# A decoder layer on one core: gates, broadcasts, branch stores and weight loads on other DMA queues

## The chip, the cores and the metric

The kernel runs on one core of one Trainium2 chip. The metric is the device time of one execution in microseconds; lower is better. The kernel before was timed three times, with a median of 1371.44 us (1367.7 to 1374.45). The profile comes from one further execution of 1372.67 us.

## What is computed

The input x has 2048 rows of 1024 float32 values. One layer is computed:

```
h    = rms_norm(x, norm_g);  proj = h @ w_in            # 1024 -> 3592 columns
fox  : 8 heads of 64, q and k normed per head, causal softmax attention with a bias
       c[t] - c[s], where c is the running sum of log_sigmoid(h @ w_f + b_f)
pool : 4 groups of 64 columns: trailing mean over 2/4/8/16 rows minus the row,
       times w_pool (64 x 64 per group), times pool_scale
sb   : 4 heads of 64, stick-breaking attention: A[t,s] = sigmoid(z_ts) prod_{s<j<t}(1 - sigmoid(z_tj)), s < t
mixed = concat(fox * silu(fg), pool * silu(pg), sb * silu(sg))
out   = x + mixed @ w_out
```

## The kernel before, in words

Rows are cut into 16 tiles of 128. Every large product is made in pairs of float16 numbers (a high and a low part), three matmuls for one. The work goes in five parts that overlap: fox heads 0 to 3 ("a"), fox heads 4 to 7 ("b"), the stick-breaking heads ("s"), the pooled branch ("p", whose tiles are strewn into the projections of s) and the output projection ("o"). Tiles and tensors carry these letters in their names: `tta` belongs to a, `ttb` to b, `tts` to s.

**One tile of attention.** `proj` (L322) makes q, k, v and the gate of a tile. `stacks` puts k and q side by side (`st`), has them transposed by a DMA from SyncE's queue (`qT`, L482) and lets GpSimd place them (L485, L487). `qk` makes scores on TensorE (L420, `sp`). In a and b VectorE adds the running sums `negc` (L754) and ScalarE takes the exponential (L764). In s ScalarE takes the sigmoid (L889), GpSimd masks the diagonal block (`affine_select`, L891, with the memset L892), VectorE multiplies along the row (the scan, L897), and GpSimd keeps the last value (`left`, L901). Then `split_t` makes high and low halves (L446 on ScalarE, L449 on VectorE) in `pp` and has them transposed by a DMA from SyncE's queue into `tt` (L451), and `pv` multiplies with v (L463 to L465). Scores run ahead of `pv` by three heads. There are four `tt` buffers.

**What lies in DRAM between the parts.** Gates go to `gat` (`keep_gate`, L509), right after the ScalarE instruction that scales them (L508). Branch results go to `mix` (`send`, L791 for a and b, L920 for s, L1013 for the pooled branch). The running sums of a tile are stored as rows (`cd`, L581) and read back, broadcast to all 128 partitions, into `negc` (`spread`, L662). The output part reads `mix` and `gat` of a tile (L1034, L1036), multiplies (L1039, L1041), has it transposed (`xTm`, L379), multiplies with w_out and adds x.

**Weights.** The weights of b, s, p and o are read twice by `raw` (L240; for p L960 and L961): once while an earlier part runs, to measure them (`wm`), and once to scale and split them (`wr`). Both go through the three buffers `raw`, which the rows of x share. The weights of p are first folded with w_pool, stored (L956) and read back; `wpT` (L945) feeds that.

**What sets the order.** Each engine has one queue and works it off in order, DMA issues included: a DMA that must wait holds back what stands behind it. The order within a queue is chosen when the program is built, by a planner that simulates the times of all instructions (`schedule_with_timeline_sim=True`); `later` and `tick` delay some steps by a number of projection steps. The constants `QW`, `QGAT`, `QSPR`, `QMIX` and others name the engine whose queue a DMA is put on ('y' SyncE, 's' ScalarE, 'g' GpSimd); `dq` looks them up.

Of the kernel before, what the change touches and what calls it, by code (L numbers as in the profile page):

```python
# [84 lines left out]
XB = 2  # L85
HPX = (0, 0, 0, 0, 0)
QB4 = 'y'
QW = 'y'
QPARK = 's'
QLX = 's'  # L90
QGAT = 'y'
QCD = 'g'
QSPR = 'y'
QMIX = 'y'
QOL = 'y'
QOR = 'y'
QOUT = 'y'
# [29 lines left out]
def hybrid(ctx: ExitStack, tc, xN, w_in, w_pT, w_out, ng, b_f, qg, kg, w_pool, p_scale, bands, out):  # L127
# [22 lines left out]
    def dq(k):  # L150
        return {"y": sy, "s": s, "g": g}[k]
# [3 lines left out]
    def later(k, fn):  # L155

        if k:
            waiting.append([k, fn])
        else:
            fn()  # L160
# [69 lines left out]
    class Weights:  # L230
# [6 lines left out]
        def raw(self, kt, a, what):  # L237
            c = self.c0 + sum(self.widths[:a])
            wr = xp.tile([P, self.widths[a]], F32, name=f"{what}{self.name}_{kt}_{a}", tag="raw", bufs=LX)
            dq(QW).dma_start(wr, self.src[kt * P:(kt + 1) * P, c:c + self.widths[a]])  # L240
            return wr
# [259 lines left out]
    def keep_gate(ph, i, j, src, iw, c):  # L501
# [5 lines left out]
        with first(HGT):  # L507
            s.activation(gt, src, AF.Copy, scale=iw[:, 0:1])  # L508
        later(GTD, lambda: dq(QGAT).dma_start(gat[j][:, c:c + 256], gt))  # L509


    class Fox:
# [143 lines left out]
        def spread(self, j):  # L656
# [4 lines left out]
            def send():  # L661
                dq(QSPR).dma_start(negc[:, :, blk], cd[j][h0:h0 + NH, :].partition_broadcast(P))  # L662
                spread_.add(f"{self.ph}_{NT - 1 - j}")
# [117 lines left out]
        def pv(self, i, h, parts, rl):  # L781
# [4 lines left out]
            if h == NH - 1:  # L786
# [3 lines left out]
                def send():  # L790
                    dq(QMIX).dma_start(mix[j][:, c:c + 256], om)  # L791
                    mixed.add((self.ph, j))
# [8 lines left out]
    class Stick(Fox):  # L801
# [102 lines left out]
        def pv(self, i, h, parts, left):  # L904
# [7 lines left out]
            if h == NH - 1:  # L912
# [6 lines left out]
                def send():  # L919
                    dq(QMIX).dma_start(mix[j][:, c:c + 256], om)  # L920
                    mixed.add((self.ph, j))
# [4 lines left out]
    class Pool:  # L926
# [9 lines left out]
        def fold(self, kt):  # L936

            w = self.w
            if kt == 0:
# [3 lines left out]
                for k in range(2):  # L943
                    self.wts.append(big.tile([P, D], F32, name=f"wpT{k}", tag="KV"[k], bufs=(KB, VB)[k]))
                    dq(QW).dma_start(self.wts[k], w_pT[k])  # L945
                self.folded = []
# [8 lines left out]
            self.folded.append(dr.tile([P, 256], F32, name=f"wf{kt}", tag=f"wf{kt}"))  # L955
            dq(QMIX).dma_start(self.folded[kt], fq)  # L956

            def raw(kt, a, what):
                wr = xp.tile([P, 512], F32, name=f"{what}p_{kt}", tag="raw", bufs=LX)
                dq(QW).dma_start(wr[:, 0:256], self.folded[kt])  # L960
                dq(QW).dma_start(wr[:, 256:512], w.src[kt * P:(kt + 1) * P, w.c0 + 256:w.c0 + 512])  # L961
                return wr
# [33 lines left out]
        def pool(self, i):  # L996
# [15 lines left out]
            def send():  # L1012
                dq(QMIX).dma_start(mix[j][:, 512:768], ym)  # L1013
                mixed.add(("p", j))
# [308 lines left out]
```

## Time and profile before

| | |
|---|---|
| median of 3 runs | 1371.44 us |
| profiled execution | 1372.67 us, its span 1371.0 us |
| mean granted TensorE clock | 0.945 |
| PE / DVE / ACT / POOL busy | 88% / 73% / 57% / 20% of the span |
| DMA queue of SyncE (q1) | 576480 packets, 232.59 MB |
| DMA queue of ScalarE (q10) | 10832 packets, 33.67 MB |
| DMA queue of GpSimd (q0) | 512 packets, 0.07 MB |

Engines: PE is TensorE's matmuls, DVE VectorE, ACT ScalarE, POOL GpSimd, SP SyncE, which only issues DMAs here. SPq, ACTq and POOLq are the issuing sides of these engines. The chain of waits goes back from the last instruction, at each step to what released it. "Issue" in it is time in which an engine waited for nothing that the profile shows. Times of a transfer "to landing" count from its issue.

### The profile page before, as it was taken

The page shows a single profiled execution, that of the slowest core. Times are in us where ns is not written, and L with a number is a line of the kernel's source. Part 1 is how long each engine was busy: PE and PEld are TensorE (multiplying, and loading weights), DVE is VectorE, ACT ScalarE, POOL GpSimd, SP SyncE. Part 2 cuts the span into 40 slices and gives each one's busy share as a digit, 9 for nine tenths or more (in the row PEclk, how much of TensorE's full clock was granted, in tenths as well). Part 3 has the DMA queues.
Part 4 walks back from the last instruction along what each step waited for, and adds up shares of the span by engine and source line. Part 5 has one row for each costly group of instructions (what it writes and reads, how often), then busy time and mean ns, then how long its engine had stood idle before and what let it go on. Part 6 is the DMA issues. An engine that isn't in the chain of part 4 may idle for free.

```text
span 1371.0 us, 27421 instructions
## 1 busy us (share of the span) xinstructions
PE 1202.0 (88%) x10380; PEld 653.9 (48%) x10380; DVE 996.3 (73%) x2069; ACT 776.5 (57%) x1457; POOL 274.0 (20%) x440
## 2 busy tenths in 40 slices
PE   6979987898896698997988879999998899878998
PEld 3445544555454354554544435545454454443443
DVE  4778876878876466878888656768786888956641
ACT  5678866868665366666667645546554556412210
POOL 0212221111011111121111034423331113303300
PEclk9989998999998899999999889999999999999999
DMA  6569998789999999989899998799798789999763
GB/s 221 162 144 209 206 197 174 171 192 196 246 197 201 218 203 192 219 168 182 173 241 187 174 208 172 170 194 182 159 196 176 159 197 259 234 266 293 210 181 93
DMA packets 587956, 268.07 MB, mean 196 GB/s; under 512 B 523440, under 2 KB 561712, under 8 KB 587824
## 3 DMA queue, kind: packets, MB, share of 16 engines
q1 hardware_dynamic: 576480, 232.59, 81.0%
q10 hardware_dynamic: 10832, 33.67, 7.8%
q8 instruction: 81, 1.33, 0.4%
q14 instruction: 51, 0.42, 0.1%
q0 software_dynamic: 512, 0.07, 0.0%
HBM read 102.60 MB, written 34.67 MB: 100 GB/s over the span
## 4 chain that ended last, share of the span: by engine, by line
PE 50%; DMA 20%; issue 10%; DVE 10%; ACT 6%; POOL 2%; SPq 1%; ACTq 0%; POOLq 0%; DVEq 0%
PE pr L322 11%; DMA ttb<-ppb 8%; DMA tta<-ppa 7%; DVE rrs L897 5%; PE pqkb L322 5%; PE pvgb L322 5%; PE pvga L322 4%; PE pqka L322 3%; PE spb L420 3%; PE pqks L322 3%; PE pvgs L322 2%; PE spa L420 2%; PE pp L322 2%; PE sps L420 1%; DMA xTm<-ppm 1%
## 5 line engine op out<-in xcount | busy, mean ns | idle before, releaser
L322 PE MATMUL pr<-wo,xTm 128*128 128x512 f16 x768 | 173.1, 387 | 15.5 <-DMA xTm<-ppm 13.8
L446 ACT CAST pps<-rrs 128x640 f16<-128x640 f32 (+7 forms) x96 | 76.1, 795 | 115.2 <-DVE rrs L897 97.9
L897 DVE TENSOR_TENSOR_SCAN rrs<-rrs 128x640 f32<-128x640 f32 (+7 forms) x64 | 105.3, 1651 | 40.8 <-POOL rrs L891 30.9
L322 PEld LDWEIGHTS <-xTm 128*128 128x128 f16 x768 | 75.4, 99 | 107.7 <-DMA xTm<-ppm 15.3
L322 PEld LDWEIGHTS <-xTs 128*128 128x128 f16 x768 | 76.0, 101 | 98.4 <-issue 22.3
L764 ACT ACTIVATE Lb<-Lb,nmb 128x640 f32<-128x640 f32 (+7 forms) x96 | 85.6, 893 | 59.6 <-DVE nmb L758 59.4
L322 PEld LDWEIGHTS <-xTb 128*128 128x128 f16 x768 | 74.1, 100 | 88.3 <-issue 10.0
L322 PEld LDWEIGHTS <-xTx 128*128 128x128 f16 x720 | 69.3, 100 | 79.0 <-issue 7.8
L322 PE MATMUL pqks<-ws,xTs 128*128 128x512 f16 x384 | 98.8, 403 | 7.1 <-DVE vo L345 5.8
L449 DVE TENSOR_TENSOR pps<-rrs,pps 128x640 f16<-128x640 f32 (+7 forms) x96 | 88.9, 937 | 20.0 <-ACT pps L446 19.5
L764 ACT ACTIVATE La<-La,nma 128x640 f32<-128x640 f32 (+7 forms) x96 | 85.4, 891 | 29.6 <-DVE nma L758 29.2
L463 PE MATMUL ob<-Vb,ttb 128*128 128x64 f16 x544 | 62.7, 199 | 44.5 <-DMA ttb<-ppb 43.7
L449 DVE TENSOR_TENSOR ppb<-Lb,ppb 128x640 f16<-128x640 f32 (+7 forms) x96 | 89.6, 952 | 11.1 <-ACT ppb L446 10.7
L449 DVE TENSOR_TENSOR ppa<-La,ppa 128x640 f16<-128x640 f32 (+7 forms) x96 | 89.2, 947 | 10.6 <-ACT ppa L446 10.2
L322 PE MATMUL pvgs<-ws,xTs 128*128 128x512 f16 x384 | 94.2, 388 | 1.6 <-DVE ym L1010 1.6
L754 DVE CUSTOM_DVE_ANT_0 Lb<-spb,negcb,c 128x640 f32<-128x640 f32 (+7 forms) x64 | 60.2, 945 | 47.7 <-PE spb L420 28.9
L322 PE MATMUL pvgb<-wb,xTb 128*128 128x512 f16 x384 | 93.0, 388 | 1.7 <-ACT gta L508 1.7
L322 PE MATMUL pqkb<-wb,xTb 128*128 128x512 f16 x384 | 92.6, 387 | 0.7 <-DVE wb L281 0.7
L889 ACT ACTIVATE rrs<-sps,nc 128x640 f32<-128x640 f32 (+7 forms) x96 | 80.0, 862 | 23.3 <-PE sps L420 23.1
L322 PE MATMUL pp<-auxp,xTp 128*128 128x512 f16 x384 | 92.2, 387 | 0.7 <-DVE vo L345 0.6
L463 PE MATMUL oa<-Va,tta 128*128 128x64 f16 x544 | 60.2, 199 | 32.7 <-DMA tta<-ppa 32.5
L420 PE MATMUL spa<-Ka,qTa 128*128 128x512 f16 (+3 forms) x320 | 78.0, 358 | 8.6 <-DVE mma L754 6.5
(312 smaller groups left out, 3053.5 us busy)
## 6 DMA issues: line engine op xcount, KB each, us to landing
xn<-in_xN_dram SPq DMA_DIRECT2D x16, 512.0 KB, 5.1
xTd<-xTx ACTq DMA_DIRECT2D x16, 512.0 KB, 4.6
xTb<-xTd ACTq DMA_DIRECT2D x16, 512.0 KB, 5.0
xTs<-xTd ACTq DMA_DIRECT2D x16, 512.0 KB, 4.5
xTp<-xTd ACTq DMA_DIRECT2D x16, 512.0 KB, 5.0
go<-gat SPq DMA_DIRECT2D x16, 512.0 KB, 7.6
mt<-mix SPq DMA_DIRECT2D x16, 512.0 KB, 5.3
xr<-in_xN_dram SPq DMA_DIRECT2D x16, 512.0 KB, 4.0
```

Of the source, the lines that this page charges most:

```text
L322: t.matmul(psum, x[:, xa, kt, :], wt[:, wa, c0:c0 + n], start=(kt == 0 and i == 0), stop=(kt == KT - 1 and i == 2))
L420: t.matmul(sp[:, b - c0 + off:e - c0 + off], qT[:, a * NH + h, :], Kc[b // 512][:, h, b % 512:b % 512 + e - b], start=(a == 0), stop=(a == ...
L446: s.copy(hi, p32)
L449: lo_eng.tensor_tensor(lo, p32, hi, ALU.subtract)
L463: t.matmul(o, tt[:, b, :], vh[:, 0:HD], start=first, stop=False)
L754: v.tensor_tensor_reduce(lt, sp, negc[:, h, c0:c1_], c1[:, 0:1], 4 * NEG if a == 0 else mm[:, a - 1:a], ALU.add, ALU.max, mm[:, a:a + 1])
L764: s.activation(ls[a], ls[a], AF.Exp, bias=nm[:, 0:1], accum_out=la[:, a, h:h + 1])
L889: s.activation(gg, sp, AF.Sigmoid, scale=self.nc2[:, 0:1])
L897: v.tensor_tensor_scan(gg, gg, gg, init, ALU.mult, ALU.bypass)
```

## The change

Four constants change; no other line does. The 64 gate stores leave SyncE's queue for ScalarE's. The 32 broadcasts, the 64 stores of branch results, the 8 stores of the folded pool weights and the 82 loads of weights leave it for GpSimd's, where so far the 16 stores of `cd` were the only DMAs.

```diff
-QW = 'y'
+QW = 'g'
...
-QGAT = 'y'
+QGAT = 's'
 QCD = 'g'
-QSPR = 'y'
-QMIX = 'y'
+QSPR = 'g'
+QMIX = 'g'
```

## Rows read from the trace of the kernel before

**Rows 1.** The page's head and its busy times.
```profile
span 1371.0 us, 27421 instructions
...
PE 1202.0 (88%) x10380; PEld 653.9 (48%) x10380; DVE 996.3 (73%) x2069; ACT 776.5 (57%) x1457; POOL 274.0 (20%) x440
```

**Rows 2.** The chain of waits by line, in 50:442, 442:800 and 800:1180.
```profile
by line: DMA tta<-ppa 24.5%; PE pvga L322 13.7%; PE pqka L322 12.0%; PE spa L420 7.8%; issue 7.0%; PE oa L463 3.1%; ACT La L764 3.1%; PE oa L464 2.4%; PE oa L465 2.4%; PE pvgb L322 2.4%; DVE La L754 2.2%; ACT ppa L446 2.1%; DMA xTd<-xTx 1.3
...
by line: DMA ttb<-ppb 30.1%; PE pqkb L322 16.8%; PE pvgb L322 14.9%; PE spb L420 12.5%; PE pvgs L322 5.2%; PE ob L463 4.2%; PE ob L464 3.4%; PE ob L465 3.4%; PE pqks L322 3.4%; DVE ppb L449 1.1%; PE pq L949 1.0%; issue 1.0%; PE spb L422 0.8
...
by line: issue 26.5%; DVE rrs L897 17.0%; PE pqks L322 7.5%; PE pp L322 7.0%; PE sps L420 4.3%; DMA tts<-pps 4.1%; ACT rrs L889 3.8%; PE pvgs L322 3.7%; POOL rrs L891 2.6%; DVE pps L449 2.4%; ACT pps L446 2.1%; PE pr L322 2.0%; POOL qTs L48
```

**Rows 3.** Waits of PE: us in total, times, longest us.
```profile
PE ob L463 <- DMA ttb<-ppb: 43.7, 21, 8.2
PE oa L463 <- DMA tta<-ppa: 32.5, 20, 4.9
...
PE os L463 <- DMA tts<-pps: 11.1, 5, 5.6
```

**Rows 4.** Waits of SP's queue, in the same columns.
```profile
SPq L451 <- PE sps L420: 54.7, 29, 10.0
SPq L451 <- DVE ppb L449: 44.1, 27, 4.5
...
SPq L662 <- DMA cd<-cr: 29.2, 11, 6.5
...
SPq L1013 <- DVE auxp L345: 25.1, 7, 6.4
SPq L509 <- ACT auxp L508: 15.4, 11, 3.8
...
SPq L240 <- DVE ppx L345: 12.9, 8, 3.2
```

**Rows 5.** Issues by line: duration ns min/median/max, first and last start us.
```profile
L509 SPq DMA_DIRECT2D gat<-gta x16: 320/447/751, 36.5 to 365.0; - x16
...
L791 SPq DMA_DIRECT2D mix<-omb x16: 327/575/1071, 450.2 to 801.7; - x16
...
L1013 SPq DMA_DIRECT2D mix<-ym x16: 319/322/1003, 894.5 to 1182.5; - x16
...
L451 SPq DMA_TRANSPOSE ttb<-ppb x94: 1188/1782/5882, 439.5 to 792.7; - x94
...
L581 POOL DMA_DIRECT2D cd<-cr x16: 518/563/702, 42.5 to 361.7; - x16
...
L401 ACTq DMA_DIRECT2D xTs<-xTd x16: 326/326/340, 673.6 to 1103.8; - x16
```

**Rows 6.** DMA issues: count, KB each, median us to landing.
```profile
gat<-auxp SPq DMA_DIRECT2D x29, 128.0 KB, 2.6
...
cd<-cr POOLq DMA_DIRECT2D x16, 4.0 KB, 3.5
```

**Rows 7.** POOL's instructions from 1032 us: start us, us, [idle before <-releaser].
```profile
1032.13 0.65 POOL L891 TENSOR_SCALAR_AFFINE_SELECT rrs<-rrs 128x128 f32<-128x128 f32 x1 [4.74 <-ACT rrs L889]
...
1036.81 0.69 POOL L901 COPY left<-rrs 128x1 f32<-128x1 f32 x1 [4.00 <-DVE rrs L897]
...
1041.09 0.29 POOL L891 TENSOR_SCALAR_AFFINE_SELECT rrs<-rrs 128x128 f32<-128x128 f32 x1 [3.01 <-ACT rrs L889]
```

**Rows 8.** SP's queue at the start of b, in the same columns.
```profile
450.80 5.60 SPq L662 DMA_DIRECT2D negcb<-cd  x6
456.51 4.99 SPq L451 DMA_TRANSPOSE ttb<-ppb  x2
...
463.56 3.85 SPq L662 DMA_DIRECT2D negcb<-cd  x6
```

**Rows 9.** Stage a: us, PE, PEld, DVE, ACT, POOL busy, clock, DMA share, GB/s.
```profile
50.00:442.00 392.00, 335.10 (x3328) 193.66 (x3327) 307.62 (x881) 275.60 (x582) 64.03 (x88) 0.94 0.92 194
```

**Rows 10.** ACT's instructions around one gate of b.
```profile
510.22 0.47 ACT L508 ACTIVATE gtb<-pvgb,iwb 128x256 f32<-128x256 f32 x1
510.59 0.82 ACT L764 ACTIVATE Lb<-Lb,nmb 128x640 f32<-128x640 f32 x1
```

## The prediction

> **What bounds the kernel now.** I read the page's busy times first, then the chain of waits cut into stages, then who waits for whom on PE and on SP, then the lengths of the issues, and last the order of POOL's and SP's instructions in two short stretches. The span is 1371.0 us and POOL is busy for 274.0 of them [rows 1]; the profiled execution itself took 1372.67 us, 1.67 more than its span and 0.1% over the median of the runs, 1371.44. The sums below are made on 1372.67.
>
> The chain of waits shows three different kernels. In stage a (50 to 442 us) the landing of the transposes tta makes up 24.5% of the chain, in stage b (442 to 800 us) that of ttb 30.1%, and the rest of stage b is almost only matmuls; neither shows POOL in its leading lines. In stage s (800 to 1180 us) tts is down to 4.1%, while 26.5% is "issue", 17.0% the scan L897 on DVE, and POOL's mask rrs L891 2.6% [rows 2]. PE agrees: it idles 43.7 us for ttb and 32.5 for tta, but only 11.1 for tts [rows 3]. So in a and b a transpose that leaves SP earlier is worth something, at most the 76 us that PE idles there. In stage s it is worth next to nothing.
>
> What that "issue" of stage s is, POOL's order tells [rows 7]: mask (L891), then the one-column copy L901 after 4.00 us of waiting for DVE's scan, then the next mask after 3.01 us of waiting for ACT's sigmoid. POOL does its work strictly in order, and the next scan cannot start before the mask. Any instruction put between L901 and L891 that waits or takes time moves the mask, and with it the scan. That is the point on which I decide.
>
> **What leaves SP.** 250 DMAs: 64 gates (to ACT), 64 stores of branches, 8 of the folded pool weights, 32 broadcasts and 82 loads of weights (to POOL). By their start times 64 of them are issued in stage a, 109 in b, 77 in s. An issue on SP takes from 0.322 us (ym) to 0.575 (omb); I take the 0.447 of gta [rows 5], which gives 29, 49 and 35 us. To these come the waits that stand ahead of them on SP, and hold back what is queued behind: 29.2 us of broadcasts for the landing of cd and 12.9 of loads for ppx, both in stage a; 25.1 of ym's stores and 15.4 of gates in stage s [rows 4]. SP gets back 71 us in a, 49 in b, 75 in s.
>
> How much of it reaches the end? If each us delays a transpose, the share of the chain that runs through transposes counts: 71 x 0.245 = 17, 49 x 0.301 = 15, 75 x 0.041 = 3, together 35 us. But SP often has nothing to send: its transposes wait 54.7 us for PE sps (a landing buffer still being read, in stage s) and 44.1 for their own data from ppb [rows 4]. When SP waits for its own data anyway, freed time is empty time. I take a little over half: **-20 us** (bounds -35 and 0). At the start of b the effect is plainest: two runs of six broadcasts hold SP for 5.60 and 3.85 us while ttb transposes wait behind them [rows 8].
>
> **What comes to POOL.** 186 DMAs. The only row of such an issue on POOL is cd's, 0.563 us for 8 rows of 512 bytes; the moved ones have 128 rows, the broadcasts 512 pieces. Bounds: 0.56 us, and the 1.782 us of a ttb transpose on SP [rows 5], which has far more pieces. I take 0.9, nearer to the row of the same queue.
>
> In stage s it is 48 of them (16 oms, 16 ym, 8 wmo, 8 wro): 43 us (27 to 86). The 25.1 us for which SP waited ahead of ym's stores goes along, since POOL's queue is as strictly ordered. Of these 68 us about 30% is on the path (issue 26.5% with the mask's 2.6%, rounded): **+20 us** (bounds 27 x 0.30 = +8, and 86 plus both waits of stage s, 40, x 0.30 = +38). Behind the waiting store stand the mask, the copy of `left` and the placing of K; DVE's scan waits for the first, ACT's and DVE's splitting for the scan, SP's transpose for these.
>
> In a and b 138 come, 124 us, where POOL is busy 64.03 of 392 us in stage a [rows 9] and off the chain. The cover is POOL's idleness; it fails where the waiting broadcasts meet the placing of K (L485, L487), for which PE's scores wait. Twelve broadcasts in a row at 0.56 to 1.78 us are 7 to 21 us in front of one K copy at the start of b. **+4 us** (0 to +15).
>
> At this price the Trainium skill speaks against the change a second time: "SBUF — State Buffer", section "SBUF: two separate sides", says that DMAs from GpSimd's queue have their descriptors written by that engine, which VectorE can lock out during certain operations, so that they start late. Stage a does not bear it out: cd's sixteen issues stay between 518 and 702 ns [rows 5] while DVE is busy 307.62 of 392 us [rows 9]. In stage s a one-column copy on POOL takes 0.69 us [rows 7], so something like it may hold there; another 0.5 us on each of the 48 issues would make it 48 x 0.5 x 0.30 = 7 us more, 1391.
>
> **What comes to ACT.** A gate's store must wait until its own ACTIVATE of 0.47 us has ended, where the next one now starts 0.37 after it [rows 10]; then the issue takes the 0.326 us of an xTs load [rows 5]. That is 0.43 us lost for each gate, 28 us for 64. ACT's leading lines hold 5.2% of the chain in a, none in b, 5.9% in s [rows 2]: **+2 us** (0 to +10, if the wait costs a us more and hits the sigmoid).
>
> **Loads of weights.** A 4 KB transfer from POOL landed after 3.5 us, a 128 KB one from SP after 2.6 [rows 6], so POOL's way is about 1 us longer. Eight loads of a layer go through three buffers, so two or three turns of it can show where a layer's load is the last thing that the projections wait for, and that is at the starts of b, s and the output: **+5 us** (0 to +10). The planner orders each queue by simulated times and will see other costs; no view tells what that does, and I leave it inside the range.
>
> Sum: -20 + 20 + 4 + 2 + 5 = +11; 1372.67 + 11 = **1384 us**.
>
> **The rivals.** *SP's relief wins.* The whole 35 us comes, POOL's issues cost 0.56 us, so stage s loses 8, and the rest is covered: 1372.67 - 35 + 8 = 1346 us. For it: PE's 76 us of idling for tta and ttb, and a b stage without ACT or POOL on its chain. Against it: SP's own waits for data. It decides if POOL's issues with 128 rows cost no more than cd's and stores seldom wait.
>
> *Nothing moves (1372, within 7).* The DMA engines are the limit in a and b: they show a share of 0.92 in stage a [rows 9], and the bytes are the same by any queue. Then a transpose that is issued earlier lands no earlier, and POOL's idle time takes the rest. Against it: they are not full, and SP's waits leave gaps. The Trainium skill gives this as a rule in "DMA: Bandwidth & Descriptors", section "Issuing engines are not separate DMA queues": all queues share the same DMA engines, and spreading over several saves issue time alone, which it calls usually small. Here that issue time is 113 us of SP's, more than the rule suggests.
>
> *POOL becomes the bound.* Its issues cost 1.78 us, the broadcasts hold up K at the start of b and in stage a: -20 + 38 + 15 + 10 + 10 = +53, 1426 us. Against it: cd's row.
>
> **How the numbers follow.** Forecast 0.44, relief wins 0.32, nothing moves 0.18, POOL the bound 0.06. The forecast's own range is 1380 to 1405 us. A difference under 0.5% (7 us) cannot be told from none here. Slower by more than that: 0.44 + 0.06 = 0.50; within: 0.18; faster: 0.32. The range that should hold the time 8 times in 10 reaches from 6 us beyond the full relief, about whose time its own cases scatter to both sides, to just short of the last rival: 1340 to 1422 us.
>
> **What would show it.** Right: in stage s DVE waits longer ahead of the scan L897 for POOL's mask, POOL shows waits at L920 and L1013, and stage s grows by 15 us or more; PE's idling for tta and ttb falls by about 20 us; issues of 128 rows on POOL take 0.7 to 1.1 us. Wrong: a stage s of unchanged length (then the masks had slack that the chain hides), PE's idling for ttb unchanged (then SP was not what held the transposes), or issues far from 0.9 us. If stage b shrinks by 30 us or more the forecast is wrong whatever stage s does.

## The result, and the profile after

The changed kernel takes 1432.21 us (median of 4 runs, 1426.32 to 1436.99) against 1371.06 us for the kernel before on the same chip: a ratio of 1.0453, with a 95% interval of 1.0417 to 1.0488. It is slower, as the forecast said, but by 61 us instead of 11, and 10 us beyond the range.

The page's head, busy times and DMA queues of the changed kernel, in the columns of [rows 1] and of the table of before:

```profile
span 1430.9 us, 27456 instructions
...
PE 1211.8 (85%) x10380; PEld 657.6 (46%) x10380; DVE 998.9 (70%) x2069; ACT 778.7 (54%) x1457; POOL 393.6 (28%) x626
...
q1 hardware_dynamic: 528192, 175.95, 66.6%
q0 software_dynamic: 15264, 48.31, 13.0%
q10 hardware_dynamic: 20048, 42.06, 9.8%
```

The work is the same. Every engine but POOL is busy for about as long as before; PE's 10 us more go with a mean granted clock of 0.934 instead of 0.945. POOL has 186 instructions more, the DMA issues, and 120 us more of busy time: 0.64 us for one. SP's queue (q1) has lost 48,288 packets and 56.64 MB. POOL's has won 14,752 packets and 48.24 MB, 3.3 KB for each, so its packets are large.

The chain of waits by line, in 50:490, 490:846 and 851:1238 of the changed kernel, which are about the stages of [rows 2], moved with their ends:

```profile
by line: DMA tta<-ppa 41.9%; PE pvga L322 11.5%; PE pqka L322 8.5%; PE spa L420 6.0%; PE pqkb L322 4.1%; issue 3.1%; PE oa L463 2.7%; PE pvgb L322 2.2%; PE oa L465 2.0%; PE oa L464 2.0%; ACT La L764 1.7%; ACT ppa L446 1.5%; DVE La L754 1.4%
...
by line: DMA ttb<-ppb 29.6%; PE pvgb L322 11.0%; PE pqkb L322 8.6%; PE spb L420 8.4%; issue 7.2%; PE pvgs L322 5.8%; PE ob L463 3.6%; PE pqks L322 3.3%; PE ob L464 3.0%; PE ob L465 3.0%; DVE ppb L449 2.7%; DVE Lb L754 2.5%; ACT Lb L764 1.1%
...
by line: issue 18.6%; DVE rrs L897 12.9%; PE pp L322 9.2%; DMA tts<-pps 7.7%; PE pvgs L322 7.0%; PE pqks L322 6.6%; PE sps L420 6.2%; POOL qTs L487 4.0%; POOL rrs L891 3.1%; ACT rrs L889 2.1%; ACT pps L446 1.7%; DMA xTp<-xTd 1.7%; DMA wro<-
```

The transposes tta were 24.5% of stage a's chain and are now 41.9%; tts went from 4.1 to 7.7%. The mask L891, on which the prediction was built, went from 2.6 to 3.1% only. PE's waits for transposes, in the columns of [rows 3]:

```profile
PE oa L463 <- DMA tta<-ppa: 79.8, 24, 19.0
PE ob L463 <- DMA ttb<-ppb: 42.7, 15, 6.6
...
PE os L463 <- DMA tts<-pps: 18.6, 8, 5.0
```

PE waits 47 us more for tta and 7.5 more for tts, with ttb unchanged. SP has 250 DMAs fewer to issue, and the transposes, 348 of the 440 that it has left, come later than before.

By the end of VectorE's last step on a tile (L778 in a and b, L915 in s), the changed kernel is 26 us behind at the last but one tile of a (438.2 against 412.3), 46 at the last (490.0 against 443.8), 44 at the end of b, 58 at the end of s (1291.3 against 1233.7) and 60 at the end of the output. So there are three losses: a slow one over stage a, a jump of 20 us at its last tile, and some 14 us in stage s. The slow one varies: at the last but one tile the two other orders of the last experiment and after_wo_sp, whose queues in stage a are the same, are 8.4 to 24.7 us behind instead of 26. What happens at the jump is seen in the timeline of the changed kernel (start us, us; what released it is in brackets):

```profile
430.92 55.27 SPq L451 DMA_TRANSPOSE tta<-ppa  x9
...
443.60 2.98 POOL L662 DMA_DIRECT2D negcb<-cd  x4 [3.80 <-DVE fb L227]
446.90 2.97 POOL L662 DMA_DIRECT2D negcb<-cd  x4 [0.32 <-issue]
```

SP issues nine transposes one behind another for 55 us, while POOL sends eight of stage b's broadcasts in 6 us. An issue that waits counts from the start of its wait; the longest took 16.7 us, and its transpose landed 31.3 us after the start. In the kernel before the longest landing of a tta transpose was 11.6. In [rows 8] SP sent six of these in 5.60 us and two transposes behind them in 4.99. The issues on POOL and ACT (ns min/median/max, first and last start) and the landings (median us), in the columns of [rows 5, 6]:

```profile
L662 POOL DMA_DIRECT2D negcb<-cd x16: 747/747/787, 443.6 to 464.4; - x16
...
L240 POOL DMA_DIRECT2D wro<-in_w_out_dram x8: 528/545/567, 973.8 to 1197.8; - x8
...
L1013 POOL DMA_DIRECT2D mix<-ym x16: 540/581/605, 950.5 to 1245.0; - x16
...
L509 ACTq DMA_DIRECT2D gat<-gta x16: 326/327/1277, 37.3 to 366.9; - x16
...
negca<-cd POOLq DMA_DIRECT2D x16, 256.0 KB, 5.3
...
negcb<-cd POOLq DMA_DIRECT2D x16, 256.0 KB, 14.6
```

An issue costs POOL 0.53 to 0.58 us, a broadcast 0.75 to 0.78. It is not the price of issues that makes this kernel slow.

### The profile page after: what moved, and what is told of

Same layout as the page of the kernel before. It is cut to its first block, busy times and chain, and to the rows that moved or that the text cites. A ratio compares the mean times of both kernels' runs of the same rounds, so it can differ in the third digit from the quotient of the medians.

```text
span 1430.9 us, 27456 instructions
## 1 busy us (share of the span) xinstructions
PE 1211.8 (85%) x10380; PEld 657.6 (46%) x10380; DVE 998.9 (70%) x2069; ACT 778.7 (54%) x1457; POOL 393.6 (28%) x626
## 4 chain that ended last, share of the span: by engine, by line
PE 46%; DMA 27%; DVE 8%; issue 8%; ACT 5%; POOL 4%; SPq 1%; ACTq 0%; POOLq 0%; DVEq 0%
DMA tta<-ppa 13%; PE pr L322 11%; DMA ttb<-ppb 7%; PE pvga L322 4%; DVE rrs L897 3%; PE pvgb L322 3%; PE pqkb L322 3%; PE pvgs L322 3%; PE pqka L322 3%; PE pqks L322 3%; PE pp L322 2%; PE spb L420 2%; DMA tts<-pps 2%; PE sps L420 2%; PE spa L420 2%
## 5 line engine op out<-in xcount | busy, mean ns | idle before, releaser
L897 DVE TENSOR_TENSOR_SCAN rrs<-rrs 128x640 f32<-128x640 f32 (+7 forms) x64 | 105.0, 1646 | 54.1 <-POOL rrs L891 39.9
L463 PE MATMUL oa<-Va,tta 128*128 128x64 f16 x544 | 62.3, 200 | 80.5 <-DMA tta<-ppa 79.8
L764 ACT ACTIVATE La<-La,nma 128x640 f32<-128x640 f32 (+7 forms) x96 | 85.4, 891 | 39.9 <-DVE nma L758 39.9
L322 PE MATMUL pqkb<-wb,xTb 128*128 128x512 f16 x384 | 98.1, 401 | 0.0
L463 PEld LDWEIGHTS <-tta 128*128 128x128 f16 x544 | 51.8, 102 | 92.2 <-DMA tta<-ppa 87.5
L889 ACT ACTIVATE rrs<-sps,nc 128x640 f32<-128x640 f32 (+7 forms) x96 | 80.0, 863 | 23.0 <-PE sps L420 15.1
```

Source lines behind the costliest of these rows:

```text
L322: t.matmul(psum, x[:, xa, kt, :], wt[:, wa, c0:c0 + n], start=(kt == 0 and i == 0), stop=(kt == KT - 1 and i == 2))
L463: t.matmul(o, tt[:, b, :], vh[:, 0:HD], start=first, stop=False)
L764: s.activation(ls[a], ls[a], AF.Exp, bias=nm[:, 0:1], accum_out=la[:, a, h:h + 1])
L889: s.activation(gg, sp, AF.Sigmoid, scale=self.nc2[:, 0:1])
L897: v.tensor_tensor_scan(gg, gg, gg, init, ALU.mult, ALU.bypass)
```

## The experiments

Times are medians; ratios are against runs of the kernel before on the same chip (1364 to 1371 us). Each diff is against the kernel named.

### One constant at a time

**only_mix** and **only_gates** (the kernel before):

```diff
-QMIX = 'y'      # only_mix
+QMIX = 'g'
-QGAT = 'y'      # only_gates, with QMIX at 'y'
+QGAT = 's'
```

> The kernel before with the 72 stores of branches and folded weights alone on POOL's queue. 'Order of POOL' (my forecast's step): in stage s the waiting stores stand ahead of the mask, +10 to +20 us, nearly all of it after 800 us, 1381 to 1391. 'Starving': 128 KB in 1 KB rows are little, 1368 to 1376. 'Planner': within 10 us.

> The kernel before with the 64 gates alone on ACT's queue. My forecast's step gives +2 us for ACT and some of SP's 20 us back: 1362 to 1374. 'Starving': 128 KB in 1 KB rows cost nothing: the same. 'Planner': within 10 us.

only_mix: 1349.69 us, 0.9874 [0.9808, 0.9941]. only_gates: 1354.2 us, 0.9926 [0.9892, 0.996]. Both are faster, and their profiled executions are 16.6 and 11.0 us ahead by the last tile of b. PE's waits for transposes don't tell why: those for ttb are 44.9 and 40.3 us against 43.7 before, those for tta 31.2 in both against 32.5. What differs in b is PE's own time. The kernel before, then only_mix (us; busy of PE, PEld, DVE, ACT, POOL; granted clock; DMA share; GB/s):

```profile
442.00:800.00 358.00, 311.56 (x2869) 173.63 (x2868) 263.52 (x596) 228.95 (x465) 55.98 (x94) 0.93 0.99 197
```
```profile
440.00:784.00 344.00, 298.24 (x2861) 167.72 (x2859) 262.44 (x592) 229.04 (x465) 74.00 (x117) 0.97 1.04 204
```

PE is busy 13.3 us less for almost the same number of matmuls, at a mean granted clock of 0.97 instead of 0.93 (0.96 in only_gates and gates_and_mix). How an emptier queue of SP would bring that, no run shows.

Stage s loses nothing with the stores on POOL: from the last tile of b to the last of s it takes 432.7 us, and 432.1 before. This is the step on which the forecast rested, so the waits are worth reading. First the kernel before (POOL's, then DVE's: us in total, times, longest us), then only_mix:

```profile
POOL left L901 <- DVE rrs L897: 134.4, 44, 6.8
POOL rrs L891 <- ACT rrs L889: 89.4, 39, 8.7
...
DVE rrs L897 <- POOL rrs L891: 30.9, 28, 5.3
```
```profile
POOL left L901 <- DVE rrs L897: 116.5, 42, 6.1
POOL rrs L891 <- ACT rrs L889: 53.7, 28, 10.4
POOL mix L920 <- DVE oms L915: 42.9, 12, 22.3
...
POOL mix L1013 <- DVE ym L1010: 17.6, 11, 4.4
...
DVE rrs L897 <- POOL rrs L891: 32.8, 27, 6.3
```

The stores of stage s do wait on POOL, 60.5 us. But POOL's waits ahead of the mask and of `left` shrink by 53.6: it waits at the stores for what it would have waited for a moment later. The scan on DVE waits for the mask 1.9 us longer in all.

The chain's "issue", from which the forecast took its share, was largely such waiting: in 800:1180 of the kernel before some 64 of its 100 us end at an instruction of POOL. The piece of 3.98 us

```profile
1032.81 3.98 issue
```

ends where `left` starts, and is the 4.00 us that POOL waits there for DVE's scan [rows 7].

**only_spread** and **only_weights** (the kernel before):

```diff
-QSPR = 'y'      # only_spread
+QSPR = 'g'
-QW = 'y'        # only_weights, with QSPR at 'y'
+QW = 'g'
```

> The kernel before with the 32 broadcasts alone on POOL's queue. Theory 'starving' (transfers with large packets on another queue take the DMA engines from the 256-byte packets of the transposes): the broadcasts of b that come in a row as stage a ends cost 20 us or more there, SP's tta transposes hang in their issues, 1390 to 1405 us. Theory 'order of POOL' (masks, K copies and stores hold each other up): POOL waits for cd ahead of K copies in stage a, 3 to 10 us, no jump at the last tile of a, 1372 to 1382. Theory 'planner' (only the new order of instructions counts): any sign, within 10 us of 1371.

> The kernel before with the 82 loads of weights alone on POOL's queue. 'Starving': each 512 KB load delays the transposes beside it, some 8 such loads in each stage, +5 to +15 us, spread over a and b, 1376 to 1386. 'Order of POOL': loads seldom wait long, 1370 to 1376. 'Planner': within 10 us of 1371, either sign.

only_spread: 1371.73 us, 1.0038 [1.0013, 1.0063]. only_weights: 1373.94 us, 1.0032 [0.9989, 1.0076]. Alone they do almost nothing, where 'starving' had expected 20 us or more from the broadcasts. The four alone multiply to 0.987. The change gives 1.045, so the loss lies in what they do together.

**gates_and_mix** (the kernel before with these two moves that made it faster):

```diff
-QGAT = 'y'
+QGAT = 's'
-QMIX = 'y'
+QMIX = 'g'
```

> The kernel before with the gates on ACT's queue and the stores of branches on POOL's, loads of weights and broadcasts left on SP's. Alone they gave ratios of 0.993 and 0.987. If the gains add up: 0.980, 1340 to 1350 us. If both come from the same relief of SP: 0.985 to 0.990. 'Planner': anything within 10 us of these.

1356.45 us, 0.9933 [0.9897, 0.9969]: faster than both kernels, but not by more than either move alone. The relief is worth 9 to 17 us whether 64, 72 or 136 DMAs leave SP; a second helping adds nothing that shows. The costs of the other two moves may have been partly paid by relief of their own in the single runs; no run separates that.

### One constant taken back

**after_spread_sp**, **after_spread_act**, **after_weights_sp**, **after_weights_act** (the changed kernel):

```diff
-QSPR = 'g'      # after_spread_sp; 's' in after_spread_act
+QSPR = 'y'
-QW = 'g'        # after_weights_sp; 's' in after_weights_act
+QW = 'y'
```

> The changed kernel with its 32 broadcasts back on SP's queue. 'Starving': the jump at the last tile of a goes, and with it 20 us or more: 1395 to 1412 us. 'Order of POOL': waits for cd go, stage s keeps its loss: 1420 to 1430. 'Planner': anything from 1371 to 1440.

> The changed kernel with its 32 broadcasts on ACT's queue: off POOL, but still not in one queue with the transposes. 'Starving' in its plain form (any second queue with larger packets takes the engines) expects the jump at the end of stage a to stay: 1420 to 1440 us. If it is a matter of what POOL's descriptors make of the packets (4 KB instead of 512 bytes), the jump shrinks: 1395 to 1415. 'Order of POOL': as with SP's queue, 1420 to 1430, without a jump.

> The changed kernel with its 82 loads of weights back on SP's queue. 'Starving': the slow growth of stage a (26 us up to its last tile but one) shrinks by 5 to 15 us, the jump at its end stays: 1417 to 1428. 'Order of POOL': 1425 to 1432.

> The changed kernel with its 82 loads of weights on ACT's queue. They were worth 46 us of the change against SP's queue (1432 to 1385). 'Starving by packets': loads have 4 KB packets on any queue and still run beside the transposes: 1415 to 1440. 'Order of POOL' (loads that wait hold back masks and K copies): the loss goes, 1380 to 1400, unless ACT's own order pays for it.

Measured: 1415.55 us, 1.0307 [1.0235, 1.038]; 1409.3 us, 1.0265 [1.0201, 1.0328]; 1385.17 us, 1.0127 [1.0092, 1.0162]; 1410.19 us, 1.0332 [1.0247, 1.0417]. The loads are the larger part. With the loads on ACT stage a is as slow as with them on POOL (24.1 us behind at its last but one tile, 26 in the changed kernel), so the transposes are slowed without POOL: another queue than SP's is enough. But stage s loses nothing with the loads on ACT (425.5 us by the measure above, 445.6 in the changed kernel). The broadcasts cost no more on ACT's queue than on SP's, as far as the intervals tell; the longest issue of a tta transpose is 7.9 us there, as in the kernel before.

### Transposes beside a bulk of other DMAs

**transposes_beside_bulk** is no layer: it has sections of 16 transposes of 512 KB on SP's queue, beside nothing, beside 4 MB of broadcasts (16 of 512-byte pieces), or beside 4 MB of plain loads (8), these on SP's, ACT's or POOL's queue:

```python
if q is not None and q is not sy:
    for b in bulks: b(q)
for i in range(16):
    if q is sy: ...            # the bulk strewn among the transposes
    tts.append(transpose(k, i))
```

> Not the layer: sixteen DMA transposes of 512 KB from SP's queue, seven times, each time after the last has landed: alone (n), with the 16 broadcasts of 256 KB (pieces of 512 bytes) between them on SP's own queue (by), all at once on ACT's (bs), all at once on POOL's (bg), and the same with 8 loads of 512 KB (4 KB rows: ly, ls, lg); the output is left as zeros. Alone some 37 us (2048 packets of 18 ns over 16 engines each). 'Starving by packets' (an engine takes a packet from each queue in turn): beside POOL's broadcasts, whose packets are 4 KB in the trace, and beside loads from either queue, a transpose goes at a tenth of its rate, 20 to 30 GB/s, until the bulk is through; beside ACT's broadcasts of 512-byte packets at some 40%; between SP's at full rate in between. The whole section takes the sum of the work, some 51 us, if no engine is left idle; more for bg if packets also wait for something, as in the changed kernel, where both queues together fell to 100 GB/s. If queues shared evenly by bytes, transposes would keep half of their rate in all of bs, bg, ls, lg.

From the first transpose's start to the end of the copy that reads the last one: 44.2 us alone; with broadcasts 63.6 on SP, 58.6 on ACT, 70.7 on POOL; with loads 54.9, 57.7 and 51.6. The issue lengths (ns min/median/max) alone, beside POOL's broadcasts and beside POOL's loads; below, the bulk's DMAs on ACT and POOL (count, KB each, median us to landing):

```profile
L153 SPq DMA_TRANSPOSE ttn<-pp x16: 2034/2468/4873, 3.0 to 42.4; - x16
...
L153 SPq DMA_TRANSPOSE ttbg<-pp x16: 1980/2539/14632, 173.1 to 239.1; - x16
...
L153 SPq DMA_TRANSPOSE ttlg<-pp x16: 2150/2462/9607, 360.2 to 406.9; - x16
...
bulk<-in_w_in_dram ACTq DMA_DIRECT2D x16, 256.0 KB, 7.2
bulk<-in_w_in_dram POOLq DMA_DIRECT2D x16, 256.0 KB, 13.4
```

The medians are alike and the longest are not: beside a bulk the first transposes crawl until it is through. From the start of the third to that of the fifth it is 5.0 us alone (7.2 to 12.2 after the first one's start), 10.6 beside ACT's broadcasts and 20.2 beside POOL's (18.3 to 38.5). The same 4 MB of broadcasts took 36.3 us on POOL's queue and 25.2 on ACT's, from the first packet to the last. The transposes' packets (queue q1: count, MB, and a share that is not used here) in 10:45 alone, in 114:139 beside ACT's broadcasts, 175:210 beside POOL's, 302:321 beside ACT's loads and 361:375 beside POOL's:

```profile
q1 hardware_dynamic: 29384, 7.41, 113.7%
...
q1 hardware_dynamic: 6670, 1.68, 45.2%
...
q1 hardware_dynamic: 5701, 1.44, 55.2%
...
q1 hardware_dynamic: 2507, 0.63, 48.5%
...
q1 hardware_dynamic: 2621, 0.66, 22.3%
```

MB by the length of each stretch, that is 212 GB/s alone, and 67, 41, 33 and 47. In the trace one packet of the broadcasts is 512 bytes and takes 27 ns on ACT's queue; on POOL's it is 4096 bytes and 199 ns; one of a load is 4096 bytes on either queue; one of a transpose is 256 bytes and 18 ns. The Trainium skill ("DMA: Bandwidth & Descriptors", section "Queues, rings and completion order") says that a DMA engine takes its queues in turn, one whole packet from each. The trace agrees in kind: beside packets of 4096 bytes the transposes keep a sixth to a fifth of their rate alone, from ACT's queue as from POOL's, and beside those of 512 bytes a third. In size it doesn't: turns of one packet each, 18 ns against 199, would leave about a twelfth beside POOL's broadcasts. The expectation's tenth is missed too, and the section with POOL's broadcasts took 20 us more than its 51. POOL's loads made the shortest section beside a bulk; what they cost is the wait of the first transposes, not the sum.

### The burst at the last tile of a

**after_negcb_sp** (the changed kernel) and **before_negcb_pool** (the kernel before):

```diff
-  dq(QSPR).dma_start(negc[:, :, blk], ...)
+  dq(QSPR if self.first else 'y').dma_start(negc[:, :, blk], ...)   # after_negcb_sp
+  dq(QSPR if self.first else 'g').dma_start(negc[:, :, blk], ...)   # before_negcb_pool
```

> The changed kernel with the broadcasts of stage b (negcb) alone back on SyncE's queue; stage a's broadcasts stay on GpSimd's. If the jump of about 20 us at the last tile of stage a is the transposes starved beside the burst of eight negcb broadcasts on POOL's queue: 1405 to 1415 us, the jump gone, the landing of negcb back near 6 us and the longest issue of a tta transpose under 8 us. If the jump is the loads of weights that are still under way at that time: 1425 to 1435 us and the jump stays. If it is a matter of the planner's order: any time between, with loss spread over the tiles.

> The kernel before with the broadcasts of stage b (negcb) alone moved to GpSimd's queue. If the burst starves the transposes by itself: 5 to 20 us slower, all of it at the last tile of stage a and the first of stage b, and the longest issue of a tta transpose over 12 us. If the burst hurts only where POOL's queue is full of loads too: within 5 us of the kernel before and no such jump.

after_negcb_sp: 1410.42 us, 1.03 [1.0231, 1.0368]; the jump is gone (15.1 us behind at the last but one tile of a, 14.8 at the last), though b then loses 10 us more. before_negcb_pool: 1384.66 us, 1.0121 [1.007, 1.0172]; 3.6 us behind at the last but one tile, 31.5 at the last, 19.9 at the end of b, 13 at the end of the kernel. The timeline of before_negcb_pool, and its landing:

```profile
423.70 28.20 SPq L451 DMA_TRANSPOSE tta<-ppa  x3
...
425.35 6.05 POOL L662 DMA_DIRECT2D negcb<-cd  x8 [1.41 <-DVE mma L754]
...
negcb<-cd POOLq DMA_DIRECT2D x16, 256.0 KB, 17.7
```

Three transposes take 28 us in a kernel in which no other DMA has changed its queue. What the queues moved in 435:450 of the kernel before, and of before_negcb_pool (q1 is SP's, q0 POOL's; packets, MB, share):

```profile
q1 hardware_dynamic: 7961, 2.91, 98.8%
```
```profile
q0 software_dynamic: 615, 2.00, 52.1%
q1 hardware_dynamic: 1323, 0.33, 38.9%
```

So the burst does it by itself; no loads of POOL's are needed. The jump goes with this queue in every kernel: from the last but one tile of a to the last, the eight with negcb on POOL fall 12 to 38 us further behind the kernel before, the nine with it on SP 2.3 at most, and after_spread_act, with 512-byte packets from ACT, 11. Not all of a jump reaches the end: after_weights_sp has the largest, and ends 11 us behind.

### The loads of weights

**after_wo_sp** (the changed kernel, only w_out's 16 loads back) and **after_negcb_wo_sp** (these and negcb):

```diff
-  dq(QW).dma_start(wr, ...)
+  dq('y' if self.name == 'o' else QW).dma_start(wr, ...)
```

> The changed kernel with the 16 loads of the output weights (wmo and wro) alone back on SyncE's queue. If the 13 to 20 us that stage s loses come from these loads standing in POOL's strictly ordered queue: 1412 to 1420 us, stage s no longer than in the kernel before, and the chain's share of the mask L891 on POOL falls. If they come from stores of branches and from gates: 1427 to 1437 us and stage s keeps its loss.

> The changed kernel with negcb's broadcasts and the loads of the output weights back on SyncE's queue. If both readings hold (the burst of broadcasts costs 20 us, the loads in POOL's order 13 to 20): 1390 to 1400 us, and the 20 to 30 us that are left are the slow growth over stage a. If only one of them holds: 1405 to 1420. If neither does and the losses are the planner's order: 1425 to 1435.

after_wo_sp: 1404.38 us over its 10 runs, which scatter from 1370.2 to 1424.4; the ratio of 1.0083 [1.0015, 1.0151] is made with the two shortest alone. All ten lie below the shortest of the changed kernel, 1426.32, so it shows the direction and no size. after_negcb_wo_sp: 1392.38 us, 1.0163 [1.0098, 1.0229]; beside after_negcb_sp, which differs from it in w_out's loads alone, that is 18 us. Stage s tells the same: from the last tile of b to its own last tile it takes 441.5 us or more in all seven kernels with w_out's loads on POOL, and 434.4 or less in the twelve without, the kernel before among them. PE's wait for tts goes along: 14.2 us or more in the seven, 13.1 or less in the twelve; 18.6 us in the changed kernel, 18.1 in after_negcb_sp, and in after_wo_sp

```profile
PE os L463 <- DMA tts<-pps: 11.1, 8, 3.0
```

in total as before [rows 3]. The scan's wait for the mask doesn't go along: 39.9 us in the changed kernel, 36.0 in after_negcb_sp, but 46.1 in after_negcb_wo_sp.

**mix_gates_negca** and **mix_gates_weights_ab** (gates_and_mix with negca, or with the weights of b and s, on POOL). The second moves 32 loads and not the 66 that its expectation names: L240 loads b's and s's weights, and the 34 loads of p's (L945, L960, L961) stay on SP:

```diff
-  dq(QSPR).dma_start(negc[:, :, blk], ...)
+  dq('g' if self.first else QSPR).dma_start(negc[:, :, blk], ...)   # mix_gates_negca
-  dq(QW).dma_start(wr, ...)
+  dq(QW if self.name == 'o' else 'g').dma_start(wr, ...)            # mix_gates_weights_ab
```

> The kernel before with gates on ScalarE's queue, the stores of branches on GpSimd's (which together gave 0.9933 of the kernel before) and the 16 broadcasts of stage a (negca) on GpSimd's. About 33 us of the loss are left unplaced between those two moves and the changed kernel with negcb and the output weights put back: they belong to negca or to the 66 other loads of weights. If the large packets of POOL's broadcasts starve the transposes of stage a one pair of broadcasts at a time: 1370 to 1385 us. If the loads do it: 1353 to 1362 us, no change from the kernel with the two moves.

> The kernel before with gates on ScalarE's queue, the stores of branches on GpSimd's, and all loads of weights but those of the output projection (66) on GpSimd's; broadcasts stay on SyncE's. If the transposes of stage a are starved beside these loads: 1370 to 1390 us with the growth in stage a. If negca does it: 1353 to 1362 us. If the two act only together: both kernels stay under 1365 us, and their effects don't sum to the 33 us.

mix_gates_negca: 1360.83 us, 0.9948 [0.9911, 0.9986], no change from gates_and_mix. mix_gates_weights_ab: 1383.79 us, 1.0109 [1.0041, 1.0178], 24 us more. Broadcasts that come one or two at a time between other work cost nothing that shows; loads do. Where, the waits of mix_gates_weights_ab show (PE's, ACT's, and min/median/max us to landing of `wrb`):

```profile
PE pqkb L322 <- ACT wb L280: 13.2, 3, 12.2
PE pqks L322 <- ACT ws L280: 7.8, 1, 7.8
...
ACT wb L280 <- DMA wrb<-in_w_in_dram: 20.5, 4, 12.7
ACT ws L280 <- DMA wrs<-in_w_in_dram: 18.0, 2, 12.6
...
DMA to landing us min/median/max: 4.5/6.9/20.7
```

and in gates_and_mix

```profile
ACT wb L280 <- DMA wrb<-in_w_in_dram: 6.8, 2, 5.9
ACT ws L280 <- DMA wrs<-in_w_in_dram: 4.9, 2, 3.1
...
DMA to landing us min/median/max: 3.5/4.9/6.0
```

where PE waits 0.9 us for `ws` and never for `wb`. On SP's queue a load of `wrb` goes between two transposes and lands in 6 us at most. On POOL's it runs beside a row of them, and one needed 20.7. ACT then waits to scale the weights, PE's queue stands at the first projection of the next stage, and 21 us go there (13.2 + 7.8).

This is not how the changed kernel loses its time: there PE never waits for `wb` or `ws`, and its tta waits are long (79.8 us, and 33.8 in mix_gates_weights_ab). The loads and the transposes meet at the same place, though. Landings of tta transposes (us min/median/max) issued about 330 to 391 us after the start in gates_and_mix, mix_gates_weights_ab and the changed kernel:

```profile
DMA to landing us min/median/max: 4.2/5.2/8.2
```
```profile
DMA to landing us min/median/max: 3.6/7.9/25.7
```
```profile
DMA to landing us min/median/max: 3.9/10.0/21.8
```

Each delays the other; which of the two PE then stands for differs from kernel to kernel.

### Another order

**after_turn12** and **after_scd6** (the changed kernel with one constant of the planner changed, no queue):

```diff
-TURN = 11     # after_turn12
+TURN = 12
-SCD = 5       # after_scd6
+SCD = 6
```

> The changed kernel with the planner's constant TURN at 12 instead of 11: the queues are those of the changed kernel, but the order of the instructions on the engines is another in most places. If the loss lies in the queues: 1420 to 1445 us. If it was an unlucky order by the planner: under 1405 us.

> The changed kernel with the planner's constant SCD at 6 instead of 5: the same queues, a somewhat different order. If the loss lies in the queues: 1420 to 1445 us. If it was an unlucky order by the planner: under 1405 us.

1433.93 us, 1.045 [1.0402, 1.0498], and 1430.93 us, 1.0419 [1.0362, 1.0476]. Two other orders on the same queues cost the same, jump and all (45 and 57 us behind at the last tile of a). So the loss as a whole is in the queues, not in an unlucky order.

## Why the prediction had the sign right and the cause wrong

The sign came out right by luck: the term that made the sum positive, +20 for stage s, is the step that failed, and without it the same sum is -9, a faster kernel. The place of the loss was wrong, and its size. The runs give this account, each step the difference of two ratios, times 1368 us:

| step | from, to | us |
|---|---|---|
| gates to ACT and stores to POOL | before, gates_and_mix | -9 |
| negca to POOL | gates_and_mix, mix_gates_negca | +2 |
| b's and s's 32 loads to POOL | gates_and_mix, mix_gates_weights_ab | +24 |
| p's 34 loads to POOL, and what the moves cost together beyond their sum | to after_negcb_wo_sp | +5 |
| w_out's loads to POOL | after_negcb_wo_sp, after_negcb_sp | +19 |
| negcb to POOL | after_negcb_sp, the changed kernel | +21 |
| sum | | +62 |

A ratio is known to 5 to 10 us and a step, the difference of two, to 5 to 14 us, so the +2 and the +5 are nothing that can be told from none.

**SP's relief, -20.** Near in size, -9 to -17 where it was measured alone, but not by the path that I named: PE's idling for the transposes hardly fell, and the gain in b came with a higher granted clock. What I didn't see either is that the first 64 DMAs bring as much as 136. The 71 and 49 us of SP's time in a and b that I counted may have been mostly empty time, as the 54.7 us of waiting for PE had hinted [rows 4]; no run shows it.

**Stage s, stores ahead of the mask, +20.** This step failed. Nothing is lost there (only_mix: 432.7 us against 432.1). I priced the share of the chain that runs through "issue" as if any wait put into POOL's order were added to it. But that "issue" was largely POOL's waiting for ACT and DVE, 224 us ahead of mask and `left` in the kernel before, and the stores' waits came out of these. Here, a wait moved to an engine that waits anyway for the same producers was not a wait added. The 14 us that stage s did lose in the changed kernel came from w_out's loads, which I had at +5 for all layers.

**POOL's issues, 0.9 us each.** They take 0.53 to 0.58, a broadcast 0.75 to 0.78. The cd row of 0.563, the row of the same queue, was the right end. The price that the Trainium skill ("SBUF — State Buffer", section "SBUF: two separate sides") would have added for VectorE's locking POOL out is not seen in the issues: L1013's sixteen lie between 540 and 605 ns. Whether it has a part in the late landings, no run shows.

**a and b, +4.** The place was right, the dozen broadcasts at the start of b, and so was the doubt about the cover. The mechanism was not: they cost POOL 12 us, but it is the transposes on SP that they hold up. The row that could have told it was [rows 9]: with DMA engines at a share of 0.92, a bulk that is sent from another queue takes its share from somebody. I used that row only for a rival in which nothing moves, as though the bytes were shared without regard to who waits. On one queue SP's order had decided who goes first; beside a second queue the transposes kept a third of their rate against 512-byte packets and a sixth to a fifth against 4096-byte ones. The rule of the Trainium skill that the rival went by ("DMA: Bandwidth & Descriptors", section "Issuing engines are not separate DMA queues") says that spreading saves issue time alone; here the second half of the spreading cost 71 us, from 0.9933 to 1.0453.

**Gates, +2.** Right: 0.327 us for an issue on ACT and no loss to be seen; only_gates is 10 us faster.

**Loads, +5.** This step failed in size: +24 for the 32 loads of b and s and +19 for w_out's 16. I priced the longer way of one DMA on a free engine, 1 us; beside transposes a load landed after up to 20.7 us. The mechanism named (a layer's last loads are what the next projections wait for, at the starts of b and s) is seen in mix_gates_weights_ab, not in the changed kernel, where PE waits for the transposes beside the loads; that loads slow transposes I had at nothing.

Of what the prediction named as signs: PE's idling for tta rose by 47 us instead of falling, and ttb's stayed, which the prediction itself had named as a sign of being wrong; stage s grew by 14, close to the 15 named, for another reason; and the rival in which POOL becomes the bound came nearest in time (1426 us) with a wrong cause.

Open: why the relief shows as clock. Why w_out's loads harm stage s from POOL's queue and not from ACT's; the runs show that they do, and that PE then waits 7 us longer for tts, but not which of POOL's instructions is late. How far the slow loss of stage a is the loads' and how far the order's, since it varies from 8 to 26 us on the same queues. Nor do the prices of negcb's burst agree: 21 us on top of the other moves, 17 alone (before_negcb_pool), and 5 together with negca (only_spread).

## What to carry to other kernels

When the DMA engines are nearly full (a share of 0.92 here), moving a transfer to an idle engine's queue doesn't make it free: it takes away the order in which transfers that are waited for went first. Move small things that nobody waits for (gates, stores of results: 9 to 17 us won here), and leave bulk that competes with latency-bound transfers in their queue. A wait moved onto an engine that already waits for the same producer cost little here; look at that engine's waits before pricing one, and move one group at a time, since the relief was won once here and the costs came on top.

## What was not expected of the hardware

- The same broadcasts go in other packets by another queue: with negca on POOL, SP's queue has 8,448 packets fewer and POOL's 1,280 more for the same 4.19 MB: 512 bytes each became 4096. They did not get faster: beside transposes 4 MB took 36.3 us on POOL's queue and 25.2 on ACT's.
- Eight broadcasts of 256 KB from POOL stretched three transposes to 28 us (before_negcb_pool); one issue took 24.0 us there, and 7.9 us at most in the kernel before.
- An issue's price on POOL is nearly flat: 0.53 to 0.58 us for a 512 KB load, 0.55 to 0.58 for a 128 KB store, 0.75 to 0.78 for a broadcast of 512 pieces (medians by group).
